# Memory attention with its products in another order: query weights times keys, and values times output weights, made once

## The chip, the cores and the metric

The kernel runs on one core of one Trainium2 chip. The metric is device time in microseconds of one execution, in the median of several runs. The engines of a core have their own instruction streams, each in order: TensorE (matrix products), VectorE, ScalarE and GpSimd (elementwise work, and GpSimd also starts DMAs), and the sync engine, which only starts DMAs here. They meet through semaphores. In the profile PE is TensorE's matmul and PEld its weight load, DVE is VectorE, ACT ScalarE, POOL GpSimd, SP the sync engine.

## The reference

One transformer layer in f32 over 512 tokens of width 2048: a hybrid mixer (mLSTM heads and forgetting attention), attention over a memory of 256 rows, and a PEER feed-forward, each with a residual and a layer norm. The change lies in the memory attention:

```python
def memory_cross_attention(x, mem, w_q, w_kv, w_o):
    q = (x @ w_q).reshape(B, S, X_HEADS, X_HD)          # 4 heads of 512
    kv = mem @ w_kv
    k = kv[..., :D_MODEL].reshape(B, -1, X_HEADS, X_HD) # 256 rows
    v = kv[..., D_MODEL:].reshape(B, -1, X_HEADS, X_HD)
    s = jnp.einsum('bshd,bmhd->bhsm', q, k) * X_HD ** -0.5
    p = jax.nn.softmax(s, -1)
    o = jnp.einsum('bhsm,bmhd->bshd', p, v).reshape(B, S, D_MODEL)
    return o @ w_o
```

## The kernel before

**Products.** Every large product is made in three matmuls of a reduced f32 format: an operand is split into a high half (ScalarE's cast) and a low half (VectorE's subtraction; every eighth on GpSimd in the first stages), and high x high, high x low and low x high are added up in PSUM. Weights come from HBM in tiles of 128 x 1024 (512 KB) on the sync queue (`load_raw`, `load_pair`, `load_w`, lines 144 to 193) through a ring of five buffers, and each is split when it has landed. All of this bears the lines 134, 137, 148 and 205 in the profile, as it sits in helpers. `group_ws` makes 512 output columns of a product with the weights stationary and the activations moving (24 matmuls a tile, as wide as there are tokens); `group_as` keeps the activations stationary and moves the weights, 512 columns wide (6 matmuls a tile and token block).

**Paths.** The 512 tokens are handled as path A (block 0, 128 tokens) and path B (blocks 1 to 3, 384 tokens), A ahead of B. A uses `group_as` with one block and turns each result where it needs it transposed; B uses `group_ws`, and `group_as` for results by token. So a weight tile costs A 6 matmuls of 512 columns, and B 24 of 384 or 18 of 512.

**Order.** The stages are generators, and the order of the instructions is written out by hand with `weave`: it runs one generator, and after so many of its steps one step of another. A step of a one-block group's end counts as one. Small follow-up work (softmax, transposes) is put in a list by `mid`, and `ride` takes one item of it after each weight tile. A scheduler then settles the order in each engine's stream. Before the change the order was: A's mLSTM heads woven with `memory` (keys and values of the memory, lines 353 to 377, stored to HBM as kmd and vmd); A's first branch and fox woven with B's mLSTM heads at a rate of 0.045; A's merge and `tail_a` (output projection, norm, memory attention, norm, expert queries) woven with the rest of B's heads, at 0.045 too; what is left of the heads; then B: first branch, fox, merge, output projection, norm, memory attention, norm; expert queries; and a last stage of 128 expert blocks.

**Gathers.** Block 0's experts are fetched by row with indirect DMAs (`gathered`, 128 rows of 8 KB a step), while B runs. `load_w` doles out these steps at a fixed rate a weight tile (`work["rate"]`, 258/315, line 1042), beginning with what is left of B's heads; in the second half of a residual none are given out. Each fetch waits for the split of the last weight tile, and VectorE takes the rows in order (lines 860 and 873).

**Memory attention before** (`cross`, lines 699 to 747). For each of the four heads the queries are projected (8 weight tiles), then three steps ride on the next head's tiles: scores and softmax by token block (L719 to L726), transposes of the probabilities (L733), and the product with the values (L741), whose split results are the 16 operands of the output projection in `residual` (32 tiles). Scores and value products are plain f32 matmuls.

Of the kernel before, what the change touches and what calls it, by code (L numbers as in the profile page):

```python
# [21 lines left out]
P = 128  # L22
# [24 lines left out]
def build(tc, I, out):  # L47
    nc = tc.nc
    with ExitStack() as ctx:
# [176 lines left out]
        def group_as(src, X, nt, evac):  # L226

            banks = [mm_bank() if nt > 1 else ma_bank() for _ in range(nt)]
            for kt in range(8):
# [8 lines left out]
                products(todo, 0, 15)  # L238
                ride()
                if kt < 7:  # L240
                    yield
# [69 lines left out]
        vmd = dp.tile([X_H, 2, P, 512], F32, tag="vmd", name="vmd")  # L311
        mkd = dp.tile([ML_H, 2, P, P], F32, tag="mkd", name="mkd")
# [40 lines left out]
        def memory(mp):  # L353
# [8 lines left out]
            for g in range(4):  # L362
                def ev_mk(s, b, g=g, k=[]):
                    if s % 2 == 0:
                        k.append(mp.tile([P, 512], F32, tag="mo", bufs=1, name=nm("mo")))
                    nc.scalar.copy(k[-1][:, (s % 2) * MEM:(s % 2 + 1) * MEM], b[:, :MEM])
                    if s % 2:
                        nc.gpsimd.dma_start(kmd[g, s // 2], k[-1])

                yield from group_ws(I["w_xkv"][g], MT, MEM, ev_mk)  # L370
            for g in range(4):
                def ev_mv(t, b, g=g):
                    v = mp.tile([P, 512], F32, tag="mo", bufs=1, name=nm("mo"))
                    nc.vector.tensor_copy(v, b)
                    nc.gpsimd.dma_start(vmd[g, t], v)

                yield from group_as(I["w_xkv"][4 + g], MT, 2, ev_mv)
# [268 lines left out]
        def residual(R, pool, src, X, W, alloc, tmp, r, out):  # L646
# [3 lines left out]
            for g in range(4):  # L650
# [8 lines left out]
                yield from group_as(W[g], X, R.nb, ev)  # L659
# [39 lines left out]
        def cross(R, pool, X1, qt, kvt, pt, opair, O):  # L699
            n, nb = R.n, R.nb  # L700
            for h in range(X_H):
                q = []

                def ev_q(s, b, q=q):
                    q.append(qt())
                    nc.scalar.activation(q[s], b[:, :n], AF.Copy, scale=X_D ** -0.5)

                yield from R.group(I["w_xq"][h], X1, ev_q)
                kt2, v2 = ([kvt(), kvt()] for _ in range(2))
                for j in range(2):  # L710
                    nc.gpsimd.dma_start(kt2[j], kmd[h, j])
                    nc.gpsimd.dma_start(v2[j], vmd[h, j])
                pr, pT = [], []

                def scores(q=q, kt2=kt2, pr=pr):
                    for qb in range(nb):
                        bank = sm_bank()
                        for c in range(4):
                            nc.tensor.matmul(bank[:, :MEM], q[c][:, qb * P:(qb + 1) * P],  # L719
                                             kt2[c // 2][:, (c % 2) * MEM:(c % 2 + 1) * MEM], start=c == 0, stop=c == 3)  # L720
                        st = pool.tile([P, 4], F32, tag="xst", bufs=4, name=nm("xst"))
                        p = pool.tile([P, MEM], F32, tag="xp", bufs=nb, name=nm("xp"))
                        nc.vector.tensor_reduce(out=st[:, 0:1], in_=bank[:, :MEM], axis=AX.X, op=ALU.max, negate=True)
                        nc.scalar.activation(p, bank[:, :MEM], AF.Exp, bias=st[:, 0:1], accum_out=st[:, 1:2])
                        nc.vector.reciprocal(st[:, 2:3], st[:, 1:2])
                        nc.vector.tensor_scalar(p, p, st[:, 2:3], None, op0=ALU.mult)  # L726
                        pr.append(p)

                def turn_p(pr=pr, pT=pT):
                    for m in range(2):  # L730
# [660 lines left out]
```

## Time and profile before

| | |
|---|---|
| median of 3 runs | 5062.73 us (5058.62 to 5063.53) |
| the profiled execution | 5072.05 us, its span 5070.3 us |
| TensorE busy | 4789.3 us (94%) |
| VectorE, ScalarE, GpSimd busy | 3728.7, 2122.9, 1270.4 us |
| mean granted clock | 0.977 |
| read from HBM, written | 1343.32 MB, 72.62 MB (279 GB/s) |

The page divides the span in 40 slices of 127 us; a digit is the busy share of one in tenths. A busy TensorE has a matmul in flight, which doesn't mean that one starts as often as could be. In tables of stretches each row has the stretch, its length, busy time and count for five engines, the granted clock, the DMA engines' busy share and the GB/s they moved. A row of a group has the line, the engine, the operation, what is written and read, the shape, the count, then busy time, mean nanoseconds of one and the idle time before them with what ended it. A row of waits has who waited for whom, the total in microseconds, how often and the longest.

### The profile page before, as it was taken

To read this page: it belongs to the slowest core of one execution; us is meant where nothing else is said; L and a number is where in the kernel's file an instruction comes from. 1 tells how busy PE (TensorE), PEld (TensorE's weight loads), DVE (VectorE), ACT (ScalarE), POOL (GpSimd) and SP (SyncE) were. 2 spreads that over 40 slices of the span, in tenths; PEclk is the share of its full clock that TensorE was granted. 3 is DMA by queue.
4 is the path that set the end of the run, shared out by engine and by line. 5 is a ranking of instruction groups with operands and counts; after the bars stand their busy time and mean duration, and the time that the engine had idled before them with its cause. 6 is when DMAs were issued, how large, how long until landed. Compare 5 with 4: busy or idle time off the path is not lost. (4 is left out here: it accounts for less than half of the span.)

```text
span 5070.3 us, 74427 instructions
## 1 busy us (share of the span) xinstructions
PE 4789.3 (94%) x28401; PEld 4397.2 (87%) x28401; DVE 3728.7 (74%) x5387; ACT 2122.9 (42%) x3046; POOL 1270.4 (25%) x1039
## 2 busy tenths in 40 slices
PE   7999999999989999998899999999989999999997
PEld 6888777777779999887888879999989999999987
DVE  6676767666977777666776565898878788787875
ACT  6556666565423233333224324434444333433332
POOL 1122223121324433323332221321001222121210
PEclk8999999999999999999999999999999999999998
DMA  7788878777689988777885774677769889898983
GB/s 247 254 283 284 279 261 276 264 249 234 225 310 357 351 326 305 275 257 260 293 323 212 258 254 162 211 256 259 281 248 364 328 336 344 328 354 321 358 302 123
DMA packets 375415, 1420.97 MB, mean 280 GB/s; under 512 B 43341, under 2 KB 104397, under 8 KB 316017
## 3 DMA queue, kind: packets, MB, share of 16 engines
q1 hardware_dynamic: 263904, 827.14, 47.3%
q0 software_dynamic: 89408, 551.06, 28.7%
q10 hardware_dynamic: 21744, 38.02, 2.0%
q8 instruction: 222, 3.64, 0.3%
q14 instruction: 137, 1.11, 0.1%
HBM read 1343.32 MB, written 72.62 MB: 279 GB/s over the span
## 5 line engine op out<-in xcount | busy, mean ns | idle before, releaser
L134 ACT CAST whi<-raw 128x1024 fp32r<-128x1024 f32 x1472 | 1533.0, 1051 | 2145.8 <-PE mm L205 823.3
L137 DVE TENSOR_TENSOR wlo<-raw,whi 128x1024 fp32r<-128x1024 f32 x1352 | 1703.7, 1271 | 698.8 <-ACT whi L134 504.6
L873 DVE SCALAR_TENSOR_TENSOR xacc<-rows,dots,xacc 128x2048 f32<-128x2048 f32 x224 | 537.3, 2399 | 220.6 <-DMA rows<-in_peer_v,eid 218.8
L860 DVE SCALAR_TENSOR_TENSOR rows<-rows,xacc 128x2048 f32<-128x2048 f32 x224 | 522.9, 2336 | 97.7 <-DMA rows<-in_peer_u,eid 97.6
L846 POOL DMA_INDIRECT rows<-in_peer_v,eid x224 | 336.0, 1500 | 1010.8 <-DVE wlo L137 389.5
L205 PE MATMUL pa<-Ch,whi 128*128 128x288 f32 x2048 | 564.8, 300 | 14.4 <-ACT ga L1223 13.0
L846 POOL DMA_INDIRECT rows<-in_peer_u,eid x224 | 309.6, 1382 | 1037.1 <-DVE rows L860 320.4
L205 PE MATMUL po<-hph,whi 128*128 128x288 f32 x2048 | 533.6, 298 | 32.6 <-ACT hph L134 27.3
L205 PE MATMUL pa<-Cl,whi 128*128 128x288 f32 x2048 | 562.8, 299 | 0.0
L205 PE MATMUL po<-hpl,whi 128*128 128x288 f32 x2048 | 533.1, 297 | 6.1 <-DVE hpl L137 6.1
L136 POOL TENSOR_TENSOR wlo<-raw,whi 128x1024 fp32r<-128x1024 f32 x120 | 309.5, 2579 | 723.8 <-ACT whi L134 444.4
L205 PE MATMUL mm<-xh,whi 128*128 128x384 f32 x1280 | 441.3, 347 | 9.1 <-DVE c L518 5.9
L205 PE MATMUL mm<-xl,whi 128*128 128x384 f32 x1280 | 433.9, 340 | 0.0
L205 PEld LDWEIGHTS po<-hph,whi 128*128 128x128 f32 x2048 | 374.8, 190 | 39.6 <-ACT hph L134 30.6
L205 PEld LDWEIGHTS pa<-Ch,whi 128*128 128x128 f32 x2048 | 389.8, 190 | 18.3 <-ACT ga L1223 14.8
L205 PEld LDWEIGHTS pa<-Cl,whi 128*128 128x128 f32 x2048 | 389.9, 190 | 1.7 <-issue 1.7
L205 PEld LDWEIGHTS po<-hpl,whi 128*128 128x128 f32 x2048 | 375.3, 190 | 7.4 <-DVE hpl L137 7.4
L205 PE MATMUL po<-hph,wlo 128*128 128x288 f32 x2048 | 349.5, 298 | 6.0 <-DVE wlo L137 6.0
L205 PE MATMUL pa<-Ch,wlo 128*128 128x288 f32 x2048 | 323.0, 297 | 3.7 <-DVE wlo L137 3.7
L205 PEld LDWEIGHTS po<-hph,wlo 128*128 128x128 f32 x2048 | 301.5, 191 | 6.5 <-DVE wlo L137 6.5
L205 PEld LDWEIGHTS pa<-Ch,wlo 128*128 128x128 f32 x2048 | 289.8, 189 | 4.7 <-DVE wlo L137 3.9
L205 PE MATMUL mm<-xh,wlo 128*128 128x384 f32 x1280 | 258.5, 337 | 5.3 <-DVE wlo L137 5.3
(440 smaller groups left out, 8778.6 us busy)
## 6 DMA issues: line engine op xcount, KB each, us to landing
raw<-in_w_in SPq DMA_DIRECT2D x512, 512.0 KB
raw<-in_uT SPq DMA_DIRECT2D x256, 512.0 KB
raw<-in_vq SPq DMA_DIRECT2D x256, 512.0 KB
raw<-in_w_xkv SPq DMA_DIRECT2D x64, 512.0 KB
raw<-in_w_br_ml SPq DMA_DIRECT2D x64, 512.0 KB
raw<-in_w_br_fx SPq DMA_DIRECT2D x64, 512.0 KB
raw<-in_w_out SPq DMA_DIRECT2D x64, 512.0 KB
raw<-in_w_xq SPq DMA_DIRECT2D x64, 512.0 KB
```

The lines of the kernel that those rows point to most:

```text
L134: nc.scalar.copy(hi, src)
L136: return nc.gpsimd.tensor_sub(lo, src, hi.bitcast(F32))
L137: return nc.vector.tensor_sub(lo, src, hi.bitcast(F32))
L205: nc.tensor.matmul(o, w if stat else x, x if stat else w, start=k == first and x is xh and not part, stop=k == last and part == 1)
L846: i = nc.gpsimd.indirect_dma_start(out=rows, out_offset=None, in_=I[table], in_offset=bass.IndirectOffsetOnAxis(ap=ei[:, k:k + 1], axis=0))
L860: nc.vector.scalar_tensor_tensor(rows, rows, 1.0, xacc, op0=ALU.mult, op1=ALU.mult, accum_out=dots[:, k:k + 1])
L873: nc.vector.scalar_tensor_tensor(xacc, rows, dots[:, k:k + 1], xacc, op0=ALU.mult, op1=ALU.add)
```

## The change

With M_h = W_q,h K_h^T and Z_h = V_h W_o,h, scores are x M_h and the output is the sum over heads of p_h Z_h. M (2048 x 256 a head) and Z (256 x 2048 a head) are made once by a new generator, `memory_products`, from the split keys and values of the memory, with the transposed query weights (`w_xqT`) and the output weights; each of these 64 weight tiles is read once instead of twice. M and Z go to HBM (`md`, `zd`, 8.4 MB each) in the shape of weight tiles, and `cross` and the second `residual` of both paths stream them as weights: 16 tiles for the scores of all heads, two heads to a group of 512 columns, and 16 tiles for the output, with the probabilities as split operands. Values are now made with the weights stationary, so that they come out turned, as the keys did.

The order changes with it. A's first branch joins its heads in being woven with `memory` (0.34); A's fox is woven with `memory_products` (0.38); B's heads start with A's merge and tail, at a rate of 0.36. The gathers' rate is 258/290. A small pool of 128 x 128 tiles has 10 buffers instead of 11.

```diff
-        def group_as(src, X, nt, evac):
+        def group_as(src, X, nt, evac, kts=8):
...
+        md = dp.tile([2, 8, P, 2, 2, MEM], F32, tag="md", name="md")
+        zd = dp.tile([4, X_H, P, 1024], F32, tag="zd", name="zd")
...
-            for g in range(4):
-                def ev_mk(s, b, g=g, k=[]):
+            for g in range(8):
+                def ev(s, b, g=g, k=[]):
...
-            for g in range(4):
-                def ev_mv(t, b, g=g):
-                    v = mp.tile([P, 512], F32, tag="mo", bufs=1, name=nm("mo"))
-                    nc.vector.tensor_copy(v, b)
-                    nc.gpsimd.dma_start(vmd[g, t], v)
-
-                yield from group_as(I["w_xkv"][4 + g], MT, 2, ev_mv)
+                yield from group_ws(I["w_xkv"][g], MT, MEM, ev)
+
+        def memory_products(zp):
+
+            def load(src):
+                t = [pair(zp, "kv", [P, 512], 8) for _ in range(2)]
+                for j in range(2):
+                    load_split(*t[j], src[j])
+                return t
...
+            K = load(kmd[0])
+            for h in range(X_H):
+                V = load(vmd[h])
+                for g in range(4):
+                    banks = [mm_bank() for _ in range(4)]
+                    for i in range(2):
+                        wh, wl = load_w(I["w_xqT"][g, 2 * h + i])
+                        todo = []
+                        for kk in range(2):
+                            kh, kl = (x[:, kk * MEM:(kk + 1) * MEM] for x in K[i])
+                            for s in range(4):
+                                c = slice(kk * 512 + s * P, kk * 512 + (s + 1) * P)
+                                todo.append((banks[s][:, :MEM], wh[:, c], wl[:, c], kh, kl, 2 * i + kk, True))
+                        products(todo, 0, 3)
+                        ride()
+                        if i == 0:
+                            yield
+                    o = out()
+                    for s in range(4):
+                        nc.scalar.activation(o[:, s * MEM:(s + 1) * MEM], banks[s][:, :MEM], AF.Copy, scale=X_D ** -0.5)
+                    for i in range(2):
+                        nc.gpsimd.dma_start(md[h // 2, 2 * g + i, :, :, h % 2],
+                                            o[:, i * 512:(i + 1) * 512].rearrange("p (k m) -> p k m", k=2))
+                    yield
+                if h < X_H - 1:
+                    K = load(kmd[h + 1])
+                for g in range(4):
+                    banks = [mm_bank() for _ in range(2)]
+                    for i in range(2):
+                        wh, wl = load_w(I["w_xo"][g, 2 * h + i])
...
+                        products(todo, 0, 3)
+                        ride()
...
+                    for m in range(2):
+                        nc.vector.tensor_copy(o[:, m * 512:(m + 1) * 512], banks[m])
+                    nc.gpsimd.dma_start(zd[g, h], o)
+                    yield
...
-        def cross(R, pool, X1, qt, kvt, pt, opair, O):
+        def cross(R, pool, X1, opair, O):
...
+            for hp in range(2):
+                pr = [None] * nb
+
+                def ev(t, b, pr=pr):
+                    st = pool.tile([P, 8], F32, tag="xst", bufs=4, name=nm("xst"))
+                    p = pr[t] = pool.tile([P, 512], F32, tag="xp", bufs=nb, name=nm("xp"))
+                    nc.vector.tensor_reduce(out=st[:, 0:2], in_=b.rearrange("p (h m) -> p h m", h=2), axis=AX.X,
+                                            op=ALU.max, negate=True)
+                    for h in range(2):
+                        m = slice(h * MEM, (h + 1) * MEM)
+                        nc.scalar.activation(p[:, m], b[:, m], AF.Exp, bias=st[:, h:h + 1],
+                                             accum_out=st[:, 2 + h:3 + h])
+                    nc.vector.reciprocal(st[:, 4:6], st[:, 2:4])
+                    for h in range(2):
+                        m = slice(h * MEM, (h + 1) * MEM)
+                        nc.vector.tensor_scalar(p[:, m], p[:, m], st[:, 4 + h:5 + h], None, op0=ALU.mult)
+
+                def turn_p(ms, pr=pr):
+                    for m in ms:
                         bank = sm_bank()
...
+                        for t in range(nb):
+                            nc.tensor.transpose(bank[:, t * P:(t + 1) * P], pr[t][:, m * P:(m + 1) * P], ident)
+                        a, b = opair()
                         nc.scalar.copy(a, bank[:, :n])
                         nc.vector.tensor_sub(b, bank[:, :n], a.bitcast(F32))
                         O.append((a, b))
...
+                yield from group_as([md[hp, kt].rearrange("p k h m -> p (k h m)") for kt in range(8)], X1, nb, ev)
+                mid(lambda f=turn_p: f((0, 1)), lambda f=turn_p: f((2, 3)))
...
-                return sa.tile([P, P], F32, tag="q", bufs=11, name=nm("aq"))
+                return sa.tile([P, P], F32, tag="q", bufs=10, name=nm("aq"))
...
-                    weave(first, mem, 52 / 77)
+                    weave(chain(first, branch_ml(A, HA, aq)), mem, 0.34)
...
-                    yield from residual(A, sa, lambda t, g: x1d[t, :, g], OA, I["w_xo"], alloc, at, r, sts)
+                    yield from residual(A, sa, lambda t, g: x1d[t, :, g], OA, zd, alloc, at, r, sts, 4)
...
+                mix = memory_products(zp)
+                weave(fox(A, a3, at, hold_y), mix, 0.38)
+                run(mix)
+                settle()
...
-            with tc.tile_pool(name="a3", bufs=1, side="right", reuse_waits="tile") as a3:
-                weave(chain(branch_ml(A, HA, aq), fox(A, a3, at, hold_y)), heads, 0.045)
-                weave(iter([2]), heads, 0)
-                settle()
-            weave(chain(merge(A, YA, GA, ac, at), tail_a()), heads, 0.045)
+            weave(chain(merge(A, YA, GA, ac, at), tail_a()), heads, 0.36)
...
-        work.update(jobs=gathered(0, 0, P, 0, lambda: work["last"]), rate=258 / 315)
+        work.update(jobs=gathered(0, 0, P, 0, lambda: work["last"]), rate=258 / 290)
...
-            run(residual(B, xp, lambda t, g: x1d[t, :, g], O, I["w_xo"], lambda i: a_tile() if i < 8 else kvt(),
-                         tmp, r, sts))
+            run(cross(B, xp, X1, lambda: pair(apool, "A", [P, B.n], 32), O))
+            run(residual(B, xp, lambda t, g: x1d[t, :, g], O, zd, lambda i: a_tile(), tmp, r, sts, 4))
```

72 lines of the change are left out of this document (22 added, 50 removed).

## The prediction

> **What bounds the kernel now.** I read the page's first two parts, then a table of stretches by stage, then single rows for prices. The page first:
>
> ```profile
> span 5070.3 us, 74427 instructions
> PE 4789.3 (94%) x28401; PEld 4397.2 (87%) x28401; DVE 3728.7 (74%) x5387; ACT 2122.9 (42%) x3046; POOL 1270.4 (25%) x1039
> PE   7999999999989999998899999999989999999997
> DVE  6676767666977777666776565898878788787875
> PEclk8999999999999999999999999999999999999998
> DMA  7788878777689988777885774677769889898983
> ```
>
> TensorE is busy nearly everywhere; no slice between the first and the last is under eight tenths. Averages over such a span can hide stages of another kind, so here is the stretch that the change touches, by stage (columns: microseconds, busy time and count of TensorE, its weight loads, VectorE, ScalarE, GpSimd, then granted clock, share of the 16 DMA engines, GB/s).
>
> ```profile
> 57.00:514.00 457.00, 439.47 (x2320) 375.91 (x2320) 316.28 (x416) 275.24 (x336) 94.27 (x76) 0.98 0.82 273
> 514.00:823.00 309.00, 300.27 (x1399) 243.63 (x1400) 212.00 (x325) 197.05 (x269) 78.44 (x76) 1.00 0.82 275
> 823.00:1292.00 469.00, 449.80 (x2047) 362.22 (x2045) 327.78 (x528) 270.15 (x393) 107.69 (x110) 0.99 0.74 251
> 1430.00:2340.00 910.00, 867.72 (x4729) 815.92 (x4730) 651.40 (x791) 284.53 (x409) 319.97 (x245) 0.98 0.84 307
> 1524.00:1778.00 254.00, 254.00 (x1467) 254.00 (x1466) 187.48 (x178) 70.51 (x77) 109.12 (x78) 1.00 0.94 352
> 2680.00:2704.00 24.00, 17.40 (x76) 14.05 (x75) 11.39 (x26) 7.98 (x10) 2.39 (x1) 0.91 0.35 110
> 2704.00:2870.00 166.00, 162.23 (x906) 153.54 (x905) 105.91 (x107) 66.29 (x113) 51.21 (x49) 0.98 0.73 264
> 2870.00:3037.00 167.00, 161.59 (x711) 130.92 (x710) 101.33 (x97) 46.10 (x58) 47.48 (x37) 1.00 0.71 256
> ```
>
> The first three rows are path A (one block of 128 tokens): first heads with the memory projections and the first branch; fox; then merge to expert queries. The fourth and fifth are path B (384 tokens) in its first branch and fox; the sixth is B's first norm, the last two its memory attention up to the second norm. What the reader is to see: in path A, whose weight tiles carry little arithmetic, TensorE is still busy 1189.5 of 1235 us, because other work is woven between. So matmul time is the currency in A too, and a tile that is merely streamed isn't free. The norm of B (24 us with 17.4 busy) is a real hole, and it stays.
>
> **Prices of a matmul.** Durations overlap, so I use start-to-start times: two stretches with one shape only, and three rows of the timeline (start, length).
>
> ```profile
> 1710.00:1760.00 50.00, 50.00 (x290) 50.00 (x289) 35.56 (x34) 12.65 (x12) 26.15 (x21) 1.00 0.97 365
> 2560.00:2660.00 100.00, 98.76 (x420) 78.25 (x419) 75.40 (x60) 27.00 (x28) 34.75 (x31) 1.00 0.84 310
> 135.92 0.28 PE L205 MATMUL mm<-mth,whi 128*128 128x256 f32 x1
> 138.80 0.40 PE L205 MATMUL ma<-whi,xh 128*128 128x512 f32 x1
> 140.18 0.28 PE L205 MATMUL mm<-mth,whi 128*128 128x256 f32 x1
> ```
>
> 384 columns: 50/290 = 0.172 us. 512 columns: 100/420 = 0.238 us in B. From 135.92 to 138.80 one weight tile's 24 matmuls of 256 columns ran: 0.120 us each. From 138.80 to 140.18 six of 512 columns: 0.230 us in A. A rule beside it: the Trainium skill, "TensorE: Matmul & The Clock Gate", section on 56 against 53.3 ns, gives a warm start-to-start time of columns over 2.4 GHz plus 2.5 ns, so an estimate of 0.216, 0.163 and 0.109 us; the rows here are some 10% above it, and by the page's figures the sum below would come to -31 instead of -25 us.
>
> **B's memory attention.** It loses the query projection (4 groups x 8 tiles x 24 matmuls of 384 columns = 768 x 0.172 = 132.4 us) and the small plain-f32 products:
>
> ```profile
> L719 PE MATMUL sm<-k,ra 128*128 128x256 f32 x96 | 22.0, 379 | 0.0
> L741 PE MATMUL sm<-t,k 128*128 128x384 f32 x64 | 22.6, 488 | 2.3 <-DVE Al L744 1.4 <-DVE Cl L744 0.9
> L733 PE MATMUL sm<-ident,xp 128*128 128x128 f32 x24 | 3.6, 274 | 1.0 <-DVE xp L726 1.0
> L719 PE MATMUL sm<-at,aq 128*128 128x256 f32 x32 | 7.9, 379 | 0.0
> L741 PE MATMUL sm<-aq,at 128*128 128x128 f32 x64 | 8.6, 278 | 1.0 <-DVE Cl L744 0.8 <-ACT aq L735 0.2
> ```
>
> Scores and values in B: 22.0 + 22.6 = 44.6 us. Transposes of the probabilities: 24 before, 24 after (2 pairs x 4 x 3), 3.6 us each way. The output projection has 32 tiles x 18 matmuls of 512 columns; afterwards 16 tiles make the scores and 16 make the output, also 18 each: 576 x 0.238 = 137 us both times. So the two stretches of 166 + 167 = 333 us lose 132.4 + 44.6 = 177 us. New on the path is the softmax of the second head pair: the old form has four heads and hides each softmax behind the next head's tiles, while now the last pair has only the first two tiles of the output projection (2 x 18 x 0.238 = 8.6 us) as cover, before tile three needs its results. That chain is, on VectorE and ScalarE, in series with weight splits and gather products. Bounds 0 (hidden) to 15 us (nearly twice that cover); I take 6, nearer to the hidden end, since today's softmax waits cost these stretches only 9 us of idle TensorE (323.8 busy of 333). Gain in B: 171 us.
>
> **A's memory attention.** Query and output projection have 64 tiles x 6 matmuls = 384; afterwards 32 tiles, 192 matmuls: -192 x 0.230 = -44.2 us. Plain products go: -7.9 - 8.6 = -16.5. Turning the queries goes, 16 transposes at about 0.15 us (3.6/24): -2.4. Together -63 us.
>
> **The products, added.** Keys: 4 heads x 4 groups x 2 tiles, 24 matmuls of 256 columns each: 32 x 24 x 0.120 = 92.2 us. Values: 32 tiles x 12 x 0.230 = 88.3 us. Total +180.5 us, all of it in A's stretch beside fox. The memory's values are now made turned, as 24 matmuls of 256 instead of 12 of 512: 32 x (2.88 - 2.76) = +4 us. B's heads, which were woven into branch, fox and tail, now all run in the tail, with about as many tiles left over: the sum doesn't change. Matmul time in A: -63 + 180.5 + 4 = +121 us; with A's idle share (45.5 of 1235, 3.7%) another 5.
>
> **Other engines in A.** The number of streamed weight tiles stays (64 fewer, 64 more), so splits don't grow overall, but they are denser beside fox.
>
> ```profile
> 514.22 307.41 SPq L148 DMA_DIRECT2D raw<-in_w_in  x152
> L134 ACT CAST whi<-raw 128x1024 fp32r<-128x1024 f32 x1472 | 1533.0, 1051 | 2145.8 <-PE mm L205 823.3
> L137 DVE TENSOR_TENSOR wlo<-raw,whi 128x1024 fp32r<-128x1024 f32 x1352 | 1703.7, 1271 | 698.8 <-ACT whi L134 504.6
> L366 ACT COPY mo<-mm 128x256 f32<-128x256 f32 x16 | 5.1, 373 | 5.5 <-DMA kmd<-mo 5.5
> L374 DVE COPY mo<-mm 128x512 f32<-128x512 f32 x8 | 5.5, 689 | 6.8 <-DMA vmd<-mo 6.7
> ```
>
> Beside fox there are now 152 tiles in 309 us: 128 of fox and 24 of B's heads. Taking the heads out (24 x 24 x 0.172 = 99 us) and the products in leaves 300 - 99 + 180.5 = 381 us of matmuls for 192 tiles, 2.0 us a tile, against 1.05 us of cast and 1.27 us of subtraction: both fit. Evacuations: 64 x 0.373 = 24 us on ScalarE, 32 x 0.689 = 22 us on VectorE, in idle time (197 and 212 busy of 309). The sync queue gets 16 loads of keys and values that wait until TensorE lets go of the old ones; the tiles ahead of them in that queue cover it. GpSimd's queue gets 48 stores behind which its share of the subtractions queues; at 78 us busy of 309 I price that at nothing, and if it isn't hidden, each late subtraction is a stall of about a copy, 48 x 0.4 = 19 us at worst. The transfers are the tight one. Before: 275 GB/s x 309 us = 85 MB. Then 40 more tiles of 0.524 MB, 16.8 MB of stored products, 4.2 MB of keys and values: 127 MB. At a full share (275/0.82 = 335 GB/s) that takes 379 us against 381 of matmuls. Bounds 0 to 30 us (a second full idle share of that stage, doubled by waits); I take 12. Path A: +121 + 5 + 12 = +138 us.
>
> **The gathers in B.** The 258 gather steps are spread over 290 tiles instead of 315, since B has 24 fewer tiles before they must be over: 0.890 instead of 0.819 a tile. Up to B's merge (about 26 + 64 + 128 tiles) that is 15 gathers more, each 128 rows of 8 KB, 1.05 MB, or 2.9 us at the 365 GB/s above: 45 us of transfer, with 84% of the DMA engines' time taken in 1430 to 2340 and 94% in its densest part. There, 60 tiles bring 12 us into 15 us of slack, and TensorE was busy for all 254 us. VectorE takes the rows in order and already waits for them:
>
> ```profile
> DVE xacc L873 <- DMA rows<-in_peer_v,eid: 107.6, 30, 8.5
> DVE rows L860 <- DMA rows<-in_peer_u,eid: 57.7, 30, 5.4
> ```
>
> Behind such a wait stand the low halves of the weights, then TensorE. Bounds 0 to 45 us; I take 8, near the lower end, as the densest row shows no matmul waiting.
>
> **Sum.** -171 (B) + 138 (A) + 8 (gathers) = -25 us. Against the profiled execution's 5072.05 us that is 5047; its time lies 9.3 us above the median of 5062.7, so in terms of the median: 5038 us. The bounds reach from all unknown terms at zero with A's idle time halved (-25 - 26 - 22 = -73) to all at their upper ends (-25 + 9 + 18 + 37 = +39).
>
> **Rivals.** First, on the other side, transfers: the gathers' extra 45 us land on the path because VectorE waits for rows. Time 5038 + 37 = 5075; it decides above 25 + 8 = 33 of the 45 us. For it: 0.94 to 0.97 of the DMA engines in the densest rows. Against it: a full TensorE in the same rows. Beside it stands a rule of the Trainium skill, "DMA: Bandwidth & Descriptors", Specifications, that a core's share of HBM is about 358 GB/s; by that rule B's densest stage would be at its limit already and every added byte would cost time. The trace's 365 GB/s is above it, so I give the case no more than 15 in 100.
>
> Second, also slower: each key group takes all four banks for only two tiles instead of eight, and its four copies (4 x 0.373 us behind a 1.05 us cast, 2.5 us) hold up the next group. 16 groups fully exposed cost 40 us: 5078. It decides at 1.6 us a group. Against it: between two steps of the products stand two or three tiles of fox, 1.4 us each. 13 in 100.
>
> Third, faster: the heads' tiles, 4.1 us each, spread through A's tail fill its idle 19 us, and transfers beside fox don't bind. Half of A's idle 45 us goes (-22) and so does the price of 12: 5003. For it: A's idle time is short waits that any ready matmul would fill. 22 in 100.
>
> **How the numbers follow.** The forecast case (5038, by itself 5015 to 5060) gets 50 in 100. About 0.2%, 10 us, is what a measurement here can tell from no change. Of the forecast's 50, 42 lie below that bound, 7 within it and 1 above; the third rival's 22 are all faster; the first gives 2 faster, 4 same and 9 slower, the second 2, 4 and 7. Faster 0.68, same 0.15, slower 0.17. The range takes in the third rival on one side and both slower ones on the other: 4993 to 5083.
>
> **What the new profile would show.** Right: B's stretch between its two norms is about 160 us long; A ends its expert queries near 1430 instead of 1292 us; the stage beside fox is some 400 us long with a DMA share near 0.95; about 450 matmuls more but less matmul time. Wrong: VectorE's waits for gathered rows in B double; TensorE idles before the products' first matmul of a group; the tail of A is longer than 540 us.

## The result and the profile after

The changed kernel takes 4984.85 us (median of 4 runs, 4973.16 to 4992.56) against 5063.13 us of the kernel before in the same comparison (4 runs, 5058.62 to 5066.74). The ratio is 0.9844, with a 95% interval of 0.9823 to 0.9865: 1.6% faster. The direction of the forecast was right. Its size was not: 78 us came where 25 were expected, and the time lies 8 us below the range.

The head of the page of the kernel after, the parts that the prediction showed of before:

```profile
span 4983.2 us, 75164 instructions
PE 4732.3 (95%) x28705; PEld 4369.2 (88%) x28705; DVE 3743.8 (75%) x5395; ACT 2137.4 (43%) x3077; POOL 1279.3 (26%) x1055
PE   7999999999998999999989999999979999999997
DVE  7766666766788777788668585988768888887875
PEclk9999999999999999999999999999999999999999
DMA  7888888765558998988789564677769989898983
```

The profiled execution took 4984.9 us, of which 4983.2 are the span. TensorE's busy time fell by 57.0 us (4789.3 to 4732.3), though it does 304 matmul records more (the prediction named about 450; its own counts add up to 304). The span fell by 87.1. So 30 us of idle TensorE went too, and that is the part to explain.

The same stages as in the prediction, now of the kernel after (columns as there: microseconds, busy time and count of TensorE, its weight loads, VectorE, ScalarE, GpSimd, then granted clock, DMA share, GB/s). The rows are: A's first heads with the memory projections and the branch; A's fox with the products; A from merge to expert queries; B's branch; B's fox; B's norm; its memory attention. The last line is the sum over all twelve stretches of the span.

```profile
57.00:475.00 418.00, 398.97 (x2448) 352.38 (x2448) 289.43 (x370) 256.77 (x324) 87.74 (x68) 0.99 0.82 284
475.00:875.00 400.00, 379.11 (x2060) 319.49 (x2061) 265.92 (x341) 253.84 (x377) 114.22 (x118) 0.99 0.87 310
875.00:1410.00 535.00, 526.19 (x2458) 438.43 (x2456) 366.60 (x667) 288.66 (x392) 116.92 (x114) 0.99 0.63 220
...
1629.00:1827.00 198.00, 195.25 (x1125) 194.51 (x1124) 148.90 (x139) 57.03 (x66) 84.36 (x59) 1.00 0.93 356
1827.00:2450.00 623.00, 613.49 (x3357) 572.32 (x3356) 481.03 (x577) 211.16 (x313) 226.94 (x184) 0.99 0.87 325
...
2780.00:2804.00 24.00, 17.22 (x74) 13.58 (x72) 11.82 (x26) 8.63 (x11) 2.39 (x1) 0.88 0.31 109
2804.00:2945.00 141.00, 136.41 (x628) 112.06 (x629) 119.81 (x131) 61.00 (x103) 54.32 (x49) 0.97 0.82 309
...
sum 4983.00, PE 4732.32 PEld 4369.20 DVE 3743.84 ACT 2137.36 POOL 1279.32; mean PE 394.36 PEld 364.10 DVE 311.99 ACT 178.11 POOL 106.61
```

Two stages of the kernel before that the prediction did not show by themselves, B's branch and B's fox, in the same columns:

```profile
1500.00:1707.00 207.00, 207.00 (x1192) 207.00 (x1192) 149.79 (x142) 59.78 (x69) 82.67 (x58) 1.00 0.93 346
1707.00:2353.00 646.00, 620.84 (x3371) 576.19 (x3370) 459.66 (x572) 209.10 (x314) 221.14 (x174) 0.99 0.81 296
```

B's fox has the same work in both kernels, yet it is 23 us shorter and its idle TensorE time fell from 25.2 to 9.5 us (646.00 - 620.84, 623.00 - 613.49), at a higher DMA share.

The following table is worked out from both traces: a stage ends when the sync queue issues a certain weight tile. These tiles are, in the order of the rows, the last of A's branch, the first of its merge, the last of its expert queries, the last of B's branch, the first of its merge, the last of its output projection, the first of its expert queries. (Expectations that count B's fox from its own first tile have 643 and 618 us where the table has 646 and 624.) The right pair of columns are second profiles of the same two programs (the runs before2 and after2 below), which show what is chance.

| stage (us) | before | after | difference | second pair | difference |
|---|---|---|---|---|---|
| A: first heads, memory projections, branch | 512 | 470 | -42 | 512, 469 | -44 |
| A: fox (after: with the products) | 312 | 405 | +94 | 313, 403 | +90 |
| A: merge to expert queries | 467 | 530 | +63 | 470, 531 | +61 |
| rest of B's heads, and B's branch | 417 | 421 | +4 | 420, 421 | +1 |
| B: fox | 646 | 624 | -22 | 646, 625 | -21 |
| B: merge and its output | 323 | 325 | +2 | 318, 324 | +6 |
| B: memory attention with the norm | 347 | 170 | -177 | 347, 170 | -177 |
| all after it | 2048 | 2038 | -10 | 2045, 2053 | +8 |

Differences are taken before rounding.

The last row as a whole shows no gain or loss: its sign turns between the pairs. (Within it the expert queries got 15 and 9 us shorter and the last stage 5 and 17 us longer.) The rest is -78 us in the first pair and -83 in the second, near the measured 78. Path A with the rest of the heads and the branch costs 119 or 108 us, B's memory attention gives 177, and B from fox to its output gives 15 to 20.

### The profile page after: what moved, and what is told of

The parts are those of the page before. It is cut to its first block, busy times and chain, and to the rows that moved or that the text cites. A ratio compares the mean times of both kernels' runs of the same rounds, so it can differ in the third digit from the quotient of the medians.

```text
span 4983.2 us, 75164 instructions
## 1 busy us (share of the span) xinstructions
PE 4732.3 (95%) x28705; PEld 4369.2 (88%) x28705; DVE 3743.8 (75%) x5395; ACT 2137.4 (43%) x3077; POOL 1279.3 (26%) x1055
## 5 line engine op out<-in xcount | busy, mean ns | idle before, releaser
L896 DVE SCALAR_TENSOR_TENSOR rows<-rows,xacc 128x2048 f32<-128x2048 f32 x224 | 523.7, 2340 | 93.1 <-DMA rows<-in_peer_u,eid 92.6
L882 POOL DMA_INDIRECT rows<-in_peer_u,eid x224 | 292.7, 1307 | 1015.1 <-DVE rows L896 341.1
```

The source lines that it names most:

```text
L882: i = nc.gpsimd.indirect_dma_start(out=rows, out_offset=None, in_=I[table], in_offset=bass.IndirectOffsetOnAxis(ap=ei[:, k:k + 1], axis=0))
L896: nc.vector.scalar_tensor_tensor(rows, rows, 1.0, xacc, op0=ALU.mult, op1=ALU.mult, accum_out=dots[:, k:k + 1])
```

## The experiments

Two theories stood after the result. By the first, the denser pace of the gathers (258/290 instead of 258/315 a weight tile) shortened B's fox. By the second, what helped was the new order of A and of B's heads, or a tail that the heads fill better. All experiments compute the full output. Each ratio is to the kernel before in the same comparison, whose median lay between 5063.61 and 5071.13 us, so a ratio is to be set against the change's 0.9844; stages are those of the profiled execution.

**The pace of the gathers alone.** In the kernel before:

```diff
-        work.update(jobs=gathered(0, 0, P, 0, lambda: work["last"]), rate=258 / 315)
+        work.update(jobs=gathered(0, 0, P, 0, lambda: work["last"]), rate=258 / 290)
```

> The kernel before, with the gathers' rate of the change alone (258/290 instead of 258/315). In the changed kernel path B's fox (first fox tile to first merge tile on the sync queue) is 618 us long instead of 643, though the forecast had the denser gathers cost 8 us. Theory (pace): the place of the gather steps among the weight tiles makes the difference; then fox in B shortens here too, by 15 to 25 us, and the whole by 10 to 25 us, to 5040 to 5053. Rival (forecast's term): denser gathers cost transfer time, the whole gets 5 to 15 us longer, 5068 to 5078. Second rival: fox in B got shorter for another reason (what precedes it); then it stays at 643 and the whole within 10 us.

Measured: 5069.67 us, ratio 1.0009 (0.9997 to 1.0021). B's fox fell from 646 to 615 us, so the pace does shorten it; but the rest of the heads and the branch rose from 417 to 428 us and the last stage (first value tile of the experts to the end) from 1367 to 1395. The whole stayed. A second profile of the same program:

> The kernel before with 258/290, for a second profile. The first showed fox 31 us shorter, the last stage 27 us longer, the whole the same. If the last stage's length belongs to this program, 1390 to 1400 again and fox about 615; if it was chance, 1365 to 1385.

Measured: 5080.61 us in one run, B's fox 618, the last stage 1386. So both shifts belong to the program and not to one execution.

The opposite, in the kernel after: the old pace up to the end of B's fox, and a faster one behind it, so that as many gathers are over in time.

```diff
-        work.update(jobs=gathered(0, 0, P, 0, lambda: work["last"]), rate=258 / 290)
+        work.update(jobs=gathered(0, 0, P, 0, lambda: work["last"]), rate=258 / 315)
...
+        work["rate"] = 1.11
```

> The changed kernel with the old gathers' rate (258/315, 0.819 a tile) up to the end of path B's fox and 1.11 a tile after it, so that the gathers end about where they do in the changed kernel. Only the pace beside heads, branch and fox differs. Theory (the pace of 0.89 is what made B's fox 20 to 30 us shorter): fox goes back from 623 to 640 to 655 us, the whole 15 to 35 us longer, 5000 to 5020. Rival (what precedes fox made it shorter): fox stays within 8 us of 623, the whole within 12 us of 4985. The denser rest may cost up to 10 us in merge and output projection under both.

Measured: 5038.48 us, ratio 0.9947 (0.9927 to 0.9968). B's fox is back at 647 us, 23 more than after. The denser rest costs 15 us more in B's memory attention (185 instead of 170). The rest of the heads and the branch together are unchanged at 421 us, so that sum doesn't hang on the pace. Path A, where no gather runs, was 9 us longer here too, so not all of the loss against the change (0.9947 against 0.9844) is the pace. And the mirror of it in the kernel before, denser up to the end of B's fox and sparser behind:

```diff
-        work.update(jobs=gathered(0, 0, P, 0, lambda: work["last"]), rate=258 / 315)
+        work.update(jobs=gathered(0, 0, P, 0, lambda: work["last"]), rate=258 / 290)
...
+        work["rate"] = 0.67
```

> The kernel before with the new rate (258/290) up to the end of B's fox and 0.67 a tile after it, so that the gathers end where they did. With 258/290 throughout, fox took 615 instead of 646 us in the profiled execution and the whole was the same within 0.2%; the last stage was 27 us longer. Theory (a gain in fox that was given back because the gathers ended elsewhere or by chance in the last stage): fox about 615 again and the whole 15 to 35 us shorter, 5030 to 5050. Rival (the last stage takes back whatever fox gains, as its transfers or its order move): fox about 615 and the whole again within 10 us of before.

Measured: 5057.64 us, ratio 0.9973 (0.9958 to 0.9987). Fox 619, merge 181 instead of 194, but the heads' rest and branch 427 and the last stage 1388. In the old kernel the pace takes 27 to 31 us out of fox, and 0 to 14 us of it arrive at the end.

What changes in B's fox is seen in the waits (engine, what it writes <- releasing engine and what was awaited: microseconds in total, times, longest). The kernel before:

```profile
POOL rows L846 <- DVE wlo L137: 205.2, 49, 14.0
DVE xacc L873 <- DMA rows<-in_peer_v,eid: 94.5, 27, 8.5
...
DVE rows L860 <- DMA rows<-in_peer_u,eid: 25.4, 14, 3.2
```

The kernel after, whose lines for the same steps are 882, 909 and 896:

```profile
POOL rows L882 <- DVE rows L896: 106.9, 31, 6.7
POOL rows L882 <- DVE wlo L137: 59.8, 15, 11.8
...
POOL rows L882 <- DVE xacc L909: 46.2, 15, 6.2
DVE xacc L909 <- DMA rows<-in_peer_v,eid: 41.9, 22, 8.9
...
DVE rows L896 <- DMA rows<-in_peer_u,eid: 3.6, 6, 1.7
```

The kernel before with the denser pace (258/290):

```profile
POOL rows L846 <- DVE rows L860: 107.3, 33, 8.2
POOL rows L846 <- DVE wlo L137: 67.4, 17, 11.4
POOL rows L846 <- DVE xacc L873: 55.1, 16, 7.1
...
DVE xacc L873 <- DMA rows<-in_peer_v,eid: 36.6, 17, 4.9
```

And the kernel after with the old pace:

```profile
POOL rows L882 <- DVE wlo L137: 227.4, 51, 9.4
DVE xacc L909 <- DMA rows<-in_peer_v,eid: 76.6, 31, 7.8
...
DVE rows L896 <- DMA rows<-in_peer_u,eid: 38.5, 17, 5.3
```

The reader is to see two ways in which a fetch is released. At the old pace GpSimd's fetch waits above all for the split of a weight tile (49 and 51 times, over 200 us), which is the pacing itself, and VectorE then waits 115 to 120 us for the rows (94.5 + 25.4, 76.6 + 38.5). At the denser pace only 15 and 17 waits are for a split, and 46 and 49 (31 + 15, 33 + 16) are for a row buffer that VectorE has just emptied; VectorE then waits 37 to 46 us for rows.

That the pacing wait itself is too late was a guess, tried by letting the fetch wait for the split of the tile before the last one. In the kernel before, and the same in the kernel after:

```diff
+            work["prev"] = work["last"]
...
-        work.update(jobs=gathered(0, 0, P, 0, lambda: work["last"]), rate=258 / 315)
+        work.update(jobs=gathered(0, 0, P, 0, lambda: work["prev"]), rate=258 / 315)
```

> The kernel before with its own gathers' rate (258/315), but each fetch waits for the split of the weight tile before the last one instead of the last. Nothing else moves. At 0.82 a tile, GpSimd's fetches in B's fox wait 205 us for a weight split (49 times), at 0.89 only 60 to 67 us, and VectorE then waits 120 against 41 to 46 us for rows. Theory (at the slow rate the fetch is released late by this wait, its product stands at a fixed place in VectorE's order, and the stream waits for the row): VectorE's waits for rows in fox fall below 60 us and fox from 646 to 615 to 630 us, at the old rate; the whole 5040 to 5075, as the last stage may move by 20 us. Rival (the rate itself matters, by where products stand among the softmax work): fox stays at 640 to 652 us.

Measured: 5101.96 us, ratio 1.0072 (1.0055 to 1.0089); fox 655. Its waits in B's fox, in the same columns (all lines are one further):

```profile
POOL rows L847 <- DVE wlo L137: 254.9, 50, 11.6
DVE xacc L874 <- DMA rows<-in_peer_v,eid: 100.6, 30, 8.3
...
DVE rows L861 <- DMA rows<-in_peer_u,eid: 39.5, 13, 5.6
```

The fetches wait as often for splits, and VectorE for rows no less: the guess falls. In this kernel an earlier release by one tile doesn't do what the denser pace does.

> The changed kernel at its own rate, with the same earlier release. Theory: its remaining 46 us of VectorE waiting for rows in fox shrink, fox from 624 to 610 to 620 us, the whole 4965 to 4985. Rival: the earlier fetches run into the densest transfers of the branch and give it back there: 4980 to 5000 with the branch above 200 us.

Measured: 4999.74 us, ratio 0.9873 (0.9856 to 0.9890). Here it does cut VectorE's wait in B's fox, and fox is 609 us; path A, the heads' rest and the stages behind fox give the 15 us back, and the whole can't be told from the change (0.9823 to 0.9865). Its waits in B's fox:

```profile
DVE xacc L910 <- DMA rows<-in_peer_v,eid: 13.0, 11, 2.9
...
DVE rows L897 <- DMA rows<-in_peer_u,eid: 4.8, 3, 2.4
```

Then a still denser pace in the kernel after, 258/270 (0.956 a tile):

```diff
-        work.update(jobs=gathered(0, 0, P, 0, lambda: work["last"]), rate=258 / 290)
+        work.update(jobs=gathered(0, 0, P, 0, lambda: work["last"]), rate=258 / 270)
```

> The changed kernel with the gathers at 258/270, 0.956 a tile, so that they end 20 tiles earlier. B's fox was 645 to 652 us at 0.80 to 0.82 a tile, 628 at 0.87, 615 to 624 at 0.89, 611 at 0.94. Theory (the denser, the fewer waits of VectorE for rows): fox about 608 to 615, memory attention of B a few us shorter, the whole 4960 to 4980. Rival (DMA engines saturate, as my first rival had it): branch and fox longer, the whole 4990 to 5010.

Measured: 5006.91 us, ratio 0.9882 (0.9858 to 0.9907). Its stretches in B's branch and fox:

```profile
1635.00:1844.00 209.00, 199.28 (x1125) 197.41 (x1125) 152.15 (x144) 57.38 (x66) 86.70 (x60) 0.98 0.89 342
1844.00:2455.00 611.00, 611.00 (x3372) 571.90 (x3371) 493.14 (x577) 211.65 (x314) 239.57 (x191) 1.00 0.92 340
```

Fox has no idle TensorE left, at a DMA share of 0.92. But the branch, the stage of B that moves the most a microsecond, rose from 198 to 209 us with 9.7 us idle, and merge from 196 to 209. What TensorE waited for most in that branch:

```profile
PE mm L205 <- DVE Hl L142: 5.6, 2, 4.2
PE mm L205 <- ACT Hh L141: 3.5, 1, 3.5
```

Hh and Hl are the halves of B's head results, which are read back here. Before the wait of 4.2 us VectorE had itself waited 2.7 us for a gathered row, and the split of Hl stood behind it: that is the first rival's case. Before the 3.5 us ScalarE waited for the transfer of Hl to land. So a loss is seen at 0.956 gathers a tile. That the sum of the transfers is its cause is not shown, as the stage's DMA share fell (0.89, from 0.93), and a run below (a_tail05) has the same stage at 0.938 gathers a tile without any idle time:

```profile
1633.00:1822.00 189.00, 189.00 (x1089) 188.41 (x1089) 145.82 (x135) 54.70 (x63) 75.71 (x57) 1.00 0.95 357
```

**The order alone, with the old products.** The kernel before, with A's fox by itself, A's branch woven with the memory projections, and all of B's remaining heads in A's tail:

```diff
-                    weave(first, mem, 52 / 77)
+                    weave(chain(first, branch_ml(A, HA, aq)), mem, 0.34)
...
+            with tc.tile_pool(name="a3", bufs=1, side="right", reuse_waits="tile") as a3:
+                run(fox(A, a3, at, hold_y))
+                settle()
...
-            with tc.tile_pool(name="a3", bufs=1, side="right", reuse_waits="tile") as a3:
-                weave(chain(branch_ml(A, HA, aq), fox(A, a3, at, hold_y)), heads, 0.045)
-                weave(iter([2]), heads, 0)
-                settle()
-            weave(chain(merge(A, YA, GA, ac, at), tail_a()), heads, 0.045)
+            weave(chain(merge(A, YA, GA, ac, at), tail_a()), heads, 0.27)
```

> The old products in the new order: A's first branch joins the heads beside the memory projections (0.34), A's fox runs alone, all of B's heads are woven into A's merge and tail (rate 0.27, so that about as many tiles are left as before), the small pool has 10 buffers. Matmul time is that of before. Theory (order fills holes): A's tail, with a head's tile at every third or fourth tile, loses some 15 us of idle TensorE, but fox alone, at 1.4 us of matmuls a tile against about 1.9 us of transfer and splitting, idles some 40 us more: A 20 to 30 us longer, the whole 5080 to 5095. Rival (matmul time is the currency everywhere): the whole within 10 us of before. Second rival: the order alone brings the gain that the forecast missed: 5010 to 5045.

Measured: 5123.7 us, ratio 1.0119 (1.0097 to 1.0141). The new order by itself costs 1.2%. A's fox alone:

```profile
469.00:740.00 271.00, 226.24 (x933) 175.08 (x934) 177.68 (x254) 162.88 (x225) 66.85 (x67) 0.91 0.83 272
```

It takes 271 us with 45 idle, at a granted clock of 0.91. It lacks the other work that covered it.

**The products not woven into fox.** In the kernel after, fox first and then the products:

```diff
-                weave(fox(A, a3, at, hold_y), mix, 0.38)
+                run(fox(A, a3, at, hold_y))
+                settle()
```

> The changed kernel with the two product matrices made after A's fox instead of beside it. Theory (tiles of A are too light to feed TensorE alone): fox alone takes about 240 us (1.9 us a tile), the products alone about 190 (2.8 us of matmuls a tile, and short waits for banks): 430 against 400 us, the whole 20 to 40 us longer, 5005 to 5025. Rival (matmul time is the currency in A as well, as the forecast had it): within 10 us of 4985.

Measured: 5040.47 us, ratio 0.9952 (0.9936 to 0.9968), some 56 us above the change. Fox, then the products:

```profile
471.00:733.00 262.00, 225.15 (x966) 177.47 (x967) 176.15 (x246) 164.98 (x231) 63.42 (x62) 0.92 0.84 284
733.00:924.00 191.00, 177.73 (x1123) 159.69 (x1122) 98.78 (x99) 94.08 (x153) 57.39 (x70) 0.99 0.80 277
```

Apart they take 262 + 191 = 453 us, woven 405. So 48 of the 56 us are here. TensorE's idle time is 50 us in the two stages against 21 woven, and its busy time 403 against 384, with a granted clock of 0.92 in fox alone. A's fox with no filler leaves TensorE idle for 37 us, and the products are that filler.

**The heads in A's tail.** In the kernel after, the heads at the old sparse rate there, with the pace of the gathers lowered to fit the tiles that are then left:

```diff
-            weave(chain(merge(A, YA, GA, ac, at), tail_a()), heads, 0.36)
+            weave(chain(merge(A, YA, GA, ac, at), tail_a()), heads, 0.045)
...
-        work.update(jobs=gathered(0, 0, P, 0, lambda: work["last"]), rate=258 / 290)
+        work.update(jobs=gathered(0, 0, P, 0, lambda: work["last"]), rate=258 / 322)
```

> The changed kernel with the heads' rate in A's tail back at 0.045 (then only about 37 of 96 head tiles run there and 59 after it; the gathers' rate is 258/322 for the 32 more tiles in B). Theory (heads fill the tail): the tail's idle share rises again from 31 to about 45 us and the whole is 10 to 20 us longer than the changed kernel, 4995 to 5005. Rival: the tail's idle time has nothing to do with it; within 8 us of 4985.

Measured: 5043.64 us, ratio 0.9945 (0.9922 to 0.9967). The tail and the rest of the heads:

```profile
876.00:1280.00 404.00, 378.77 (x1702) 307.30 (x1701) 282.20 (x471) 228.38 (x324) 90.51 (x93) 0.97 0.71 241
1280.00:1658.00 378.00, 363.22 (x1727) 308.62 (x1726) 322.90 (x577) 131.81 (x166) 141.32 (x100) 0.98 0.78 288
```

The change has 754 us from the start of A's tail to B's branch (875 to 1629), so this run has 28 more here. Of these, 11 are idle TensorE (40 us against 29), which is what the heads in the tail are worth as cover; the other 17 are busy time, which this run doesn't explain. Another 21 us are B's fox, 645 us at this pace of 0.80, and some 20 lie in the stages after B's memory attention, 18 of them in the last (1391). The other way, the heads denser than in the change:

```diff
-            weave(chain(merge(A, YA, GA, ac, at), tail_a()), heads, 0.36)
+            weave(chain(merge(A, YA, GA, ac, at), tail_a()), heads, 0.5)
...
-        work.update(jobs=gathered(0, 0, P, 0, lambda: work["last"]), rate=258 / 290)
+        work.update(jobs=gathered(0, 0, P, 0, lambda: work["last"]), rate=258 / 275)
```

> The changed kernel with B's heads at 0.5 instead of 0.36 in A's tail; about 15 fewer of their tiles are left for B, and the gathers' rate is 258/275 for that. Theory (head tiles fill the tail; 0.045 cost 28 us in tail and rest of heads together): the returns diminish, as at 0.36 the tail idles 31 of 535 us; tail and rest of heads together 735 to 755 us instead of 754, the whole 4970 to 4990. Rival (every tile moved into the tail gains as much as between 0.045 and 0.36, 28 us for 33 tiles): 12 us shorter, 4970 to 4975 and fox in B shorter still. Second rival: gathers at 0.94 a tile saturate the DMA engines in B's branch and fox: 4995 to 5020.

Measured: 5008.49 us, ratio 0.9893 (0.9866 to 0.9919). Tail and rest take 758 us, no less than the change's 754; fox 611, given back in merge (205) and output (138). Past the change's values nothing more was found here.

**Half of the change.** Only the query weights times the keys are made once; the values, the probabilities times them and the output projection stay as before (pace 258/298):

```diff
-                for g in range(4):
-                    banks = [mm_bank() for _ in range(2)]
...
-                    nc.gpsimd.dma_start(zd[g, h], o)
...
-            run(cross(B, xp, X1, lambda: pair(apool, "A", [P, B.n], 32), O))
-            run(residual(B, xp, lambda t, g: x1d[t, :, g], O, zd, lambda i: a_tile(), tmp, r, sts, 4))
+            run(cross(B, xp, X1, kvt, lambda: tmp(), lambda h: cpair() if h == 3 else pair(apool, "A", [P, B.n], 32), O))
+            run(residual(B, xp, lambda t, g: x1d[t, :, g], O, I["w_xo"], lambda i: a_tile() if i < 8 else kvt(), tmp, r, sts))
```

> Half of the change: only query weights times keys is made once, and scores use it; values and output projection are as before (plain products with the probabilities, 32 tiles of output weights), in the new order, with half as many product tiles beside fox and the gathers' rate 258/298. By matmul time the keys' half is worth: A -22 -2 -8, B -132 -22 +69, products +92, so -25 us, and the values' half -28 us. Theory (in the new order fox needs the product tiles as filler, and fox alone costs 60 us more than its matmuls): this kernel lacks half of the filler and half of the gain, 5010 to 5050. Rival (the two halves add up by matmul time alone): 28 us above the changed kernel, 5008 to 5018, with A's fox at 310 us.

Measured: 5065.42 us, ratio 0.9989 (0.9976 to 1.0003): half of the change gains nothing that can be told. A's fox with half of the products, A's tail, and B's attention:

```profile
470.00:812.00 342.00, 304.79 (x1682) 256.95 (x1683) 213.57 (x290) 214.13 (x327) 98.16 (x103) 0.96 0.85 293
812.00:1391.00 579.00, 571.22 (x2694) 476.45 (x2694) 381.84 (x656) 317.69 (x437) 122.14 (x119) 0.99 0.67 221
2751.00:3008.00 257.00, 244.60 (x1067) 193.90 (x1066) 167.25 (x175) 91.77 (x142) 73.15 (x62) 0.97 0.67 243
```

B's attention does gain 90 us (347 to 257). But path A ends at 1391 instead of 1292 us: fox with half of the products is 342 us, 37 of them idle, as long an idle time as with no filler (a_alone). That fits b_order and a_alone: the new order takes the heads away from fox, and half of the products doesn't make up for them.

**The two programs once more.** For what is chance between executions:

> The kernel before, unchanged, for a second profile: how far do stages move between two executions of one program? The last stage (first value tile to the end) was 1367 us before and 1373 to 1397 in nine variants that don't touch it. If it is chance, it lies anywhere in 1365 to 1395 here; if it belongs to the program (its order in each engine's stream), within 5 us of 1367. Fox in B should be 640 to 652 again.

> The changed kernel, unchanged, for a second profile: fox in B 618 to 630 us again if the shorter fox belongs to the program; last stage 1373 within 5 us if it belongs to the program, 1365 to 1395 if it is chance.

Measured: 5072.63 and 4997.69 us, each in one run; their stages are the right columns of the table above.

## Why the prediction was right in direction and wrong in size

**B's memory attention, -171: right, 6 us too small.** The stage gave 177. The stretch between the two norms is 154 us long (2804 to about 2958), where about 160 were named. The term of 6 us for the last softmax was too high. TensorE's busy time fell by 174 us in that stage and its idle time by 4. The step that turns the second pair's probabilities stalls TensorE for 2 us, as the groups of the trace of after show (line, engine, operation, out <- in, shapes and count, busy time and mean ns of one, idle time before them with what ended it):

```profile
L776 PE MATMUL sm<-ident,xp 128*128 128x128 f32 x32 | 5.2, 274 | 2.1 <-DVE Al L779 2.1
```

**Path A, +138: about 19 to 30 us too high.** It came to 119 and 108 in the two pairs, with the heads' rest and B's branch, to which tiles moved. The matmul part was right: in the first pair busy TensorE rose by 117 us there, where +121 was named, and over the whole span it fell by 57.0 us, where the terms -177 and +121 make -56. What was too high is the idle time: 17 us more were named (5 + 12), some 2 came. The products' stage is 405 us, as named (400), and its idle time did rise by 12 us (8.7 to 20.9), the size of the term for transfers, though its DMA share is 0.87 and not 0.95. (The 335 GB/s taken for a full share was too low: B's branch moved 356 at 0.93.) But the tail, with all heads in it, lost 10 us of idle time (19.2 to 8.8), which the forecast left out and the third rival had. A ended its expert queries near 1410 us, named was 1430. The second rival, a bank's turnover at each key group, is refuted. The groups of the products in that stage:

```profile
L205 PE MATMUL mm<-kvh,whi 128*128 128x256 f32 x256 | 63.1, 285 | 1.4 <-ACT whi L134 0.8 <-ACT zo L405 0.5
...
L205 PE MATMUL mm<-whi,kvh 128*128 128x512 f32 x107 | 42.7, 399 | 2.4 <-ACT whi L134 2.4
```

TensorE was held up by the copies out of the banks (zo, line 405) for 0.5 us in all, where that rival needed 1.6 us a group.

**"The gathers in B", +8: the step that failed, in sign.** B from fox to its output gave 15 to 20 us where 8 were to be lost, so this term missed by 23 to 28. The row that it went by, 1524 to 1778, is mostly the branch, where TensorE had no idle time to lose; fox, which follows, had 25.2 us. The prediction saw VectorE's waits for rows and took more gathers a tile to make them longer. In fact they fell from 119.9 to 45.5 us in B's fox, and the stage's idle TensorE time from 25.2 to 9.5. The runs show the pace as the cause, both ways: fox falls by 27 to 31 us with the denser pace in the old kernel (b_rate290, b_pace290) and rises by 23 with the old pace in the new one (a_pace315). Losses of the kind that the bounds of 0 to 45 us stood for are seen only further up, at 0.956 a tile (a_rate270). Here the range was wrong as well: it took in no gain, though no row excluded one, since fox had a DMA share of 0.81 and room for 25.2 us of idle TensorE to vanish, and the prediction's own row from 1430 to 2340 shows 42 us of it (910.00 - 867.72).

Why the denser pace lets VectorE meet its rows in time is not settled. It isn't simply that each fetch is released one tile earlier: that did nothing in the old kernel (b_prev), though in the new one it cut the wait from 45.5 to 17.8 us (a_prev). How far the scheduler sets a product behind its fetch differs between the programs, and that was not tried by itself. Nor is it settled why the old kernel gives the gain back in its last stage (1386 to 1395 instead of 1367 us) and the new one at most in part (1373 and 1383). The pace alone doesn't explain that stage: at the sparsest pace, in a_tail045, it took 1391 us.

**The sum.** By parts in the first pair, measured against forecast: attention 6 us better, path A with the moved tiles 19 better, gathers 28 better, 53 in all. 25 + 53 is the 78 measured. That it meets the medians so well is in part luck, as the second pair adds up to 83.

**The rivals.** The first (transfers on the path, 5075) is refuted for this change; at a pace 7% higher one stall of its kind is seen (4.2 us in a_rate270). Of the rule named beside it, 358 GB/s a core (the Trainium skill, "DMA: Bandwidth & Descriptors", Specifications): B's branch moved 356 GB/s with TensorE busy 195.25 of 198 us, and 357 in a_tail05 with TensorE busy throughout; no run moved more over that whole stage. That fits a limit near the rule's figure better than the prediction granted, though 365 GB/s were seen over 50 us of the kernel before. But no run shows added bytes costing time at it: where the stage got longer (a_rate270), it moved 342. The third (5003) came nearest in time, partly for its reason: the tail was filled, but TensorE's waits for the cast of a weight tile beside fox did rise (10.4 us, from 1.9; that transfers caused them isn't shown), and the gain in B's fox was not in it. The figures by the matmul rule (the Trainium skill, "TensorE: Matmul & The Clock Gate", section on 56 against 53.3 ns) gave -31 instead of -25, and differ by less than the idle terms missed. The measured prices lie 6 to 10% above that rule, not all some 10%.

## What to carry to other kernels

When work is moved, price the cover and not only the work: fox of path A alone is 262 to 271 us with TensorE busy 225 to 226, and the products, 191 us alone, cost only 143 beside it (405 - 262). So what stands beside it gets some 40 to 50 us free, and half of a change may pay the whole loss of the old cover. Where a stream of prefetches is paced and its consumer waits on it, a denser pace may shorten the wait as well as lengthen it: give such a term both signs, and look for idle time and free DMA share in that stage's own row. A gain seen in one stage is no gain until the end of the span shows it; an edit of the pace that saved 31 us in fox was worth nothing in the whole of the old kernel.

## What the runs showed that was not expected

- More gathers in the same stretch went with fewer waits for them: at 0.82, 0.89 and 0.956 a weight tile VectorE waited 120, 46 and 10 us in B's fox (94.5 + 25.4 before, 41.9 + 3.6 after, 7.0 + 2.5 in a_rate270), at DMA shares of 0.81, 0.87 and 0.92. The two runs with other rates of the heads fit: 148 us at 0.80 (a_tail045), 1.5 at 0.938 (a_tail05).
- Stages far from an edit moved by 19 to 29 us, reproducibly (the last stage 1395 and 1386 us in the old kernel with the denser pace, 1367 and 1366 without), while two profiles of one program differ by some 2 us in most stages, 9 at the most in the merge and 10 in the last, and by up to 15 over all that follows B's memory attention.
- In stretches with TensorE 83 to 86% busy the granted clock was 0.91 and 0.92 (fox alone in b_order and a_alone), against 0.99 in the same stage with the products beside it.
